# Expert weights in four consecutive rows per partition, with two places of double size

## The chip, the cores and the metric

The kernel runs on one core of one Trainium2 chip. The metric is the device time of one execution in microseconds (us). Three runs of the kernel before are shown, and one profiled execution, from which every duration below is taken.

## The reference, cut to what matters

Two networks are chained. The first has two layers; each has a mixer (attention and a gated part, which are not touched here) and a mixture of experts in which every expert chooses its tokens. Layer 0 runs it on 256 latent and 256 context tokens apart, layer 1 on the latent tokens alone. The second network has two layers of attention and MLP and is not touched.

```python
def expert_choice_ffn(h, w_router, w1, w3, w2):
    n_tok, d = h.shape[1], h.shape[2]
    cap = EC_FACTOR * n_tok // N_EXPERTS
    aff = jax.nn.softmax(jnp.einsum('bnd,de->bne', h, w_router).astype(jnp.float32), axis=-1)
    gate, idx = lax.top_k(jnp.swapaxes(aff, 1, 2), cap)
    xs = jax.vmap(lambda hb, ib: hb[ib])(h, idx)
    a = jnp.einsum('becd,edf->becf', xs, w1)
    b = jnp.einsum('becd,edf->becf', xs, w3)
    y = jnp.einsum('becf,efd->becd', jax.nn.silu(a) * b, w2) * gate[..., None].astype(h.dtype)
    ...
```

There are 16 experts in each of the two layers, with w1, w3 and w2 of 1024 x 1024 floats (4 MiB) each: 2 x 16 x 3 x 4 MiB = 384 MiB that are read once. Each expert takes 32 tokens of a stream.

## The kernel before, in words

`build` chains the parts: the even mixer, `moe(0)`, the odd mixer, `moe(1)`, then the second network. All weights are loaded by `wload` (L153), which SyncE (SP) issues in program order on one queue; a load waits on SP until its place is free, and every load behind it waits too. Outside of `moe`, places are taken in turn from `self.slots`: a ring of four buffers of 8 KB per partition, and one more buffer from the second stage on.

In `moe` (L1000 to L1250) a list, `self.plan`, gives the place of each load: the four ring buffers, then buffers that the earlier stages have left (`b3`, the layer's own small rings `rb`, the six of `big`), single tiles that are not yet wanted (`early`, the two halves of a load in two tiles `om`; `spare`, the later groups' `xs`), and then the same again. A load is 1 MiB: 256 rows of an expert matrix, with two consecutive rows in each partition (`paired=True`, "(p k) n -> p k n"), so a packet is 8 KB.

Since partition p holds rows 2p and 2p+1, everything that is multiplied with these rows is put in the same order:

- `gather` (L1092) builds `xs`, the experts' tokens with the features on the partitions, by matmuls whose stationary operand is `paired(...)`: every second float of a token's row (L1097).
- `paired_gains` (L1258) brings the norm's gain and shift into the same order, by two groups of four small matmuls (L1267), each with a copy to `gb` (L1269). It stands at the start of `moe`, among the last vector operations of the router (`rstd`, L274 to L280; the logits `lgS`, L527).
- `expert` (L1111) multiplies `xs` with w1 into `pa` and with w3 into `pb` (L1121), takes silu and the product, transposes the hidden rows with stride 2 (`hps`, L1130) into `hT`, and multiplies with w2 into `py` (L1140).

In layer 0 a group of matmuls has 64 token rows and takes the 1024 columns in two halves (HF = 2); in layer 1 it has 32 rows and four quarters (HF = 4). Every float32 matmul is two records in the trace.

Of the kernel before, what the change touches and what calls it, by code (L numbers as in the profile page):

```python
# [8 lines left out]
F32 = mybir.dt.float32  # L9
# [71 lines left out]
class Net:  # L81
# [11 lines left out]
    def open(self, ctx, ring):  # L93
# [3 lines left out]
        self.slots = [(ctx.enter_context(tc.tile_pool(name="ring", bufs=ring)), "w", ring)] * ring  # L97
        self.turn = 0
        self.plan = []
# [25 lines left out]
    def load_gains(self, t, names):  # L125

        nc = self.nc
        if t:
            st = self.wk.tile([P, P], F32, tag="kz", name="gs", bufs=2)
        else:  # L130
            pool, tag, bufs = self.slots[0]
            st = pool.tile([P, 2048], F32, tag=tag, name="gs", bufs=bufs)[:, :P]
# [20 lines left out]
    def wload(self, src, kk, n, paired=False):  # L153

        slot = self.plan.pop(0) if self.plan else None
        if slot is None:
            slot = self.slots[self.turn % len(self.slots)]
            self.turn += 1
        if type(slot) is list:
            for k, t in enumerate(slot):  # L160
                self.nc.sync.dma_start(out=t, in_=src.rearrange("(p k) n -> p k n", p=P)[:, k, :])
            return slot
        if type(slot) is tuple:
            pool, tag, bufs = slot
            t = pool.tile([P, 2048], F32, tag=tag, name="w", bufs=bufs)
        else:
            t = slot
        v = t[:, :kk * n].rearrange("p (k n) -> p k n", k=kk)
        self.nc.sync.dma_start(out=v, in_=src.rearrange("(p k) n -> p k n" if paired else "(k p) n -> p k n", p=P))
        return v  # L170
# [826 lines left out]
    def moe(self, L, streams):  # L997
# [6 lines left out]
        with ExitStack() as st:  # L1004
# [10 lines left out]
            self.paired_gains(gb, L)  # L1015
            ga, b3 = gb[:, 0], gb[:, 1]
            base = self.slots
            self.slots = base + [(self.big, "b%d" % i, 1) for i in (0, 1, 2, 4, 5, 6)]
            self.slots = self.slots[:5] + [(rb[-1], "w", n[1])] * n[1] + self.slots[5:] + [(rb[0], "w", n[0])] * n[0]
            self.turn = 0  # L1020
# [88 lines left out]

            def expert(e, xs, y4, hooks={}):  # L1110
                pa = ab.tile([P, CW], F32, tag="ab", name="pa")  # L1111
                pb = ab.tile([P, CW], F32, tag="ab", name="pb")
                for dst, nm in ((pa, "exp_w1"), (pb, "exp_w3")):
                    for k0 in range(0, NK, 2):
                        if (nm, k0) in hooks:
                            hooks[nm, k0]()
                        w = self.wload(A[nm][L, e, k0 * P:(k0 + 2) * P, :], 2, D, True)
# [711 lines left out]
```

## Time and profile before

| | |
|---|---|
| median of 3 runs | 2309.74 us (2308.86 to 2312.27) |
| profiled execution | 2310.7 us |
| its span, first to last instruction | 2308.6 us |
| TensorE busy | 2054.4 us, 89% |
| VectorE, ScalarE, GpSimd busy | 43%, 32%, 9% |
| DMA, the weights' queue | 71.1% of 16 engines, 275 GB/s mean |
| granted clock, mean | 0.939 |

The experts of layer 0 run from about 293 to 741 us, those of layer 1 from about 958 to 1395 us. The table's shares are averages over stages with different limits, so the two expert stretches are read by themselves. A window's row gives each engine's busy time in it, the granted clock, the mean busy share of the 16 DMA engines (it can read slightly over 1) and the GB/s moved.

### The profile page before, as it was taken

The page shows a single profiled execution, that of the slowest core. Times are in us where ns is not written, and L with a number is a line of the kernel's source. Part 1 is how long each engine was busy: PE and PEld are TensorE (multiplying, and loading weights), DVE is VectorE, ACT ScalarE, POOL GpSimd, SP SyncE. Part 2 cuts the span into 40 slices and gives each one's busy share as a digit, 9 for nine tenths or more (in the row PEclk, how much of TensorE's full clock was granted, in tenths as well). Part 3 has the DMA queues.
Part 4 walks back from the last instruction along what each step waited for, and adds up shares of the span by engine and source line. Part 5 has one row for each costly group of instructions (what it writes and reads, how often), then busy time and mean ns, then how long its engine had stood idle before and what let it go on. Part 6 is the DMA issues. An engine that isn't in the chain of part 4 may idle for free.

```text
span 2308.6 us, 31250 instructions
## 1 busy us (share of the span) xinstructions
PE 2054.4 (89%) x12759; PEld 1340.9 (58%) x12759; DVE 987.7 (43%) x1744; ACT 747.9 (32%) x1226; POOL 206.3 (9%) x254
## 2 busy tenths in 40 slices
PE   6999899999887899786666658999999999999998
PEld 3666644433222667543222225777899888778997
DVE  4456532132211756410110105456664555566545
ACT  4345210110000444100000004665454457655443
POOL 1001000000000210000000002111111102021112
PEclk8999999999999899887786778999999999999999
DMA  8547589999999476999999996435555544355552
GB/s 327 201 154 257 220 332 421 418 418 421 422 421 398 157 258 244 354 420 421 420 421 421 421 421 235 147 104 162 174 186 179 201 164 142 124 171 177 183 199 74
DMA packets 156746, 634.10 MB, mean 275 GB/s; under 512 B 12270, under 2 KB 16955, under 8 KB 101691
## 3 DMA queue, kind: packets, MB, share of 16 engines
q1 hardware_dynamic: 155354, 630.53, 71.1%
q8 instruction: 100, 1.64, 0.3%
q10 hardware_dynamic: 1248, 1.58, 0.2%
q14 instruction: 44, 0.35, 0.0%
HBM read 631.02 MB, written 1.05 MB: 274 GB/s over the span
## 4 chain that ended last, share of the span: by engine, by line
PE 65%; DMA 26%; DVE 5%; issue 2%; ACT 1%; POOL 1%; SPq 0%; DVEq 0%; ACTq 0%; POOLq 0%
DMA w<-in_exp_w_dram 25%; PE ps L242 8%; PE ps L244 8%; PE ps L243 8%; PE ups L1419 8%; PE acc L1419 7%; PE py L1140 3%; PE pa L1121 3%; PE pb L1121 3%; PE mod L408 2%; PE gps L1097 2%; PE S L546 2%; PE Z L1419 1%; DMA w<-in_mod_w_dram 1%; PE S L1419 1%
## 5 line engine op out<-in xcount | busy, mean ns | idle before, releaser
L182 DVE TENSOR_TENSOR wl<-w,wh 128x1024 fp32r<-128x1024 f32 (+2 forms) x333 | 409.1, 1250 | 167.2 <-ACT wh L181 158.7
L181 ACT CAST wh<-w 128x1024 fp32r<-128x1024 f32 (+2 forms) x337 | 338.1, 1027 | 171.5 <-PE acc L1419 69.6
L1121 PE MATMUL pb<-w,xs 128*32 128x256 f32 (+1 forms) x1504 | 208.7, 533 | 61.6 <-DMA w<-in_exp_w_dram 60.9
L1121 PE MATMUL pa<-w,xs 128*32 128x256 f32 (+1 forms) x1536 | 212.0, 521 | 43.2 <-DMA w<-in_exp_w_dram 42.3
L1140 PE MATMUL py<-w,ht 128*32 128x256 f32 (+1 forms) x1520 | 199.7, 515 | 41.9 <-DMA w<-in_exp_w_dram 27.6
L1126 DVE TENSOR_TENSOR sa<-sa,pb 128x512 f32<-128x512 f32 (+1 forms) x32 | 17.7, 555 | 412.7 <-PE pb L1121 359.0
L242 PE MATMUL ps<-wh,hT 128*128 128x512 f32 x468 | 187.5, 401 | 0.4 <-DVE g L1402 0.4
L243 PE MATMUL ps<-wl,hT 128*128 128x512 f32 x468 | 183.6, 392 | 0.0
L244 PE MATMUL ps<-wh,hT 128*128 128x512 f32 x468 | 183.3, 392 | 0.0
L1121 PEld LDWEIGHTS pb<-w,xs 128*32 128x32 f32 (+1 forms) x1504 | 69.3, 135 | 189.0 <-issue 88.3
L1121 PEld LDWEIGHTS pa<-w,xs 128*32 128x32 f32 (+1 forms) x1536 | 68.2, 132 | 162.1 <-issue 78.7
L1419 PE MATMUL acc<-wh,u 128*128 128x512 f32 x512 | 160.3, 390 | 0.0
L1140 PEld LDWEIGHTS py<-w,ht 128*32 128x32 f32 (+1 forms) x1520 | 67.4, 131 | 155.2 <-issue 72.9
L1125 ACT ACTIVATE sa<-pa 128x512 f32<-128x512 f32 (+1 forms) x32 | 15.7, 490 | 431.5 <-PE pa L1121 431.3
L1419 PE MATMUL ups<-hh,wl 128*128 128x256 f32 x512 | 145.0, 283 | 0.0
L1419 PE MATMUL ups<-hh,wh 128*128 128x256 f32 x512 | 145.0, 283 | 0.0
L1419 PE MATMUL ups<-hl,wh 128*128 128x256 f32 x512 | 144.9, 283 | 0.0
L1154 DVE TENSOR_TENSOR y<-py,om 32x512 f32<-32x512 f32 (+1 forms) x96 | 53.2, 554 | 174.8 <-PE py L1140 172.9
L1419 PEld LDWEIGHTS acc<-wh,u 128*128 128x128 f32 x512 | 96.1, 188 | 19.6
L242 PEld LDWEIGHTS ps<-wh,hT 128*128 128x128 f32 x468 | 88.2, 188 | 21.9 <-issue 2.1
L1419 PE MATMUL acc<-wl,u 128*128 128x512 f32 x256 | 99.8, 390 | 0.0
L244 PEld LDWEIGHTS ps<-wh,hT 128*128 128x128 f32 x468 | 88.3, 189 | 18.9
(446 smaller groups left out, 3327.1 us busy)
## 6 DMA issues: line engine op xcount, KB each, us to landing
w<-in_exp_w_dram SPq DMA_DIRECT2D x380, 1024.0 KB, 19.8
w<-in_w_in_dram SPq DMA_DIRECT2D x60, 1024.0 KB, 5.2
w<-in_mod_w_dram SPq DMA_DIRECT2D x48, 1024.0 KB, 6.0
w<-in_w_up_dram SPq DMA_DIRECT2D x32, 1024.0 KB, 5.3
w<-in_w_down_dram SPq DMA_DIRECT2D x32, 1024.0 KB, 6.7
w<-in_w_o_dram SPq DMA_DIRECT2D x8, 1024.0 KB, 5.1
w<-in_ev_w_in_dram SPq DMA_DIRECT2D x7, 1024.0 KB
w<-in_od_w_in_dram SPq DMA_DIRECT2D x6, 1024.0 KB, 7.2
```

Source lines behind the costliest of these rows:

```text
L181: nc.scalar.copy(vh, raw)
L182: (eng or nc.vector).tensor_tensor(vl, raw, vh.bitcast(F32), op=ALU.subtract)
L242: nc.tensor.matmul(ps[:, :nb], a, wh[:, cols], start=j == 0, stop=False)
L243: nc.tensor.matmul(ps[:, :nb], a, wl[:, cols], start=False, stop=False)
L244: nc.tensor.matmul(ps[:, :nb], b, wh[:, cols], start=False, stop=j == kt - 1)
L408: nc.tensor.matmul(ps[32 * j:32 * j + 32, :], self.sc[:, k, :], w[:, 0, j * 512:(j + 1) * 512], start=k == 0, stop=k == NK - 1, skip_group ...
L546: nc.tensor.matmul(Sv[e][:, :nk], a[:, t * P:(t + 1) * P], b, start=i == 0, stop=masks is None and i == len(qk[e]) - 1, skip_group_check=True)
L1097: nc.tensor.matmul(ps[:, s * nj + j, :], self.paired(streams[s][:, t, :], k + j), OH[s, t][:, g * P:(g + 1) * P], start=t == 0, stop=t == ...
L1121: nc.tensor.matmul(dst[h * T:(h + 1) * T, :], xs[:, k0 + kk, e % 4, :], wv[:, h * CW:(h + 1) * CW], start=k0 + kk == 0, stop=k0 + kk == NK ...
L1140: nc.tensor.matmul(py[n * T:(n + 1) * T, :], a, w[:, kk, n * CW:(n + 1) * CW], start=c == 0, stop=c == NK - 1, skip_group_check=True)
L1154: nc.vector.tensor_tensor(y4[s][r:r + 32, n * CW:(n + 1) * CW], py[p0:p0 + 32, :], late["m5"][s][r:r + 32, n * CW:(n + 1) * CW], op=ALU.mult)
L1419: nc.tensor.matmul(ps, a, b, start=start, stop=stop, skip_group_check=True)
```

## The change

- The ring is one tile. Two double-size places, `self.wide`, lie over its four buffers; a load to one of them takes 2 MiB in one go, with four consecutive rows in each partition, so a packet is 16 KB.
- Each expert matrix half (512 rows) is one `wquad`: either one load to a wide place, or two loads of 1 MiB to two other places, each with two of the partition's four rows: pieces of 8 KB, 16 KB apart in memory.
- `quads_of` pairs the other places in the order of the list; an odd one is kept and paired with the next narrow place, behind the wide ones that stand between.
- Everything multiplied with these rows follows the new order: the stationary operand of the gather takes every fourth float (`quad_cols`, 192 matmuls), the hidden transposes take stride 4 in layer 0 and 2 in layer 1, and in layer 1 the moving operand of w1 and w3 is read in pairs of floats out of every four (`hid_cols`, 1024 matmuls). `quad_gains` has two copies, 16 matmuls with 32 columns of the identity, and two copies.

Of the weight loads, 52 are wide (28 in layer 0, 24 in layer 1) and 276 are narrow, beside the half loads to `om`. In layer 0 the two wide loads stand, counted in MiB of expert weights from the layer's first, at 0, 18, 32, 48, 62 and then every 12 or 14 up to 178. The last loads of both layers are narrow.

```diff
-        self.slots = [(ctx.enter_context(tc.tile_pool(name="ring", bufs=ring)), "w", ring)] * ring
+        ring_t = ctx.enter_context(tc.tile_pool(name="ring", bufs=1)).tile([P, ring * 2048], F32, name="ring")
+        self.slots = [ring_t[:, i * 2048:(i + 1) * 2048] for i in range(ring)]
+        self.wide = [ring_t[:, i * 2048:(i + 2) * 2048] for i in range(0, ring, 2)]
...
+    def wquad(self, src):
+
+        place = self.quads.pop(0)
+        v = src.rearrange("(p k) n -> p k n", k=4)
+        if type(place) is not tuple:
+            t = place.rearrange("p (k n) -> p k n", k=4)
+            self.nc.sync.dma_start(out=t, in_=v)
+            return [t[:, k, :] for k in range(4)]
+        rows = []
+        for slot in place:
+            k = len(rows)
+            if type(slot) is list:
+                for i, t in enumerate(slot):
+                    self.nc.sync.dma_start(out=t, in_=v[:, k + i, :])
+                rows += slot
+            else:
+                t = self.slot_tile(slot).rearrange("p (k n) -> p k n", k=2)
+                self.nc.sync.dma_start(out=t, in_=v[:, k:k + 2, :])
+                rows += [t[:, i, :] for i in range(2)]
+        return rows
+
+    @staticmethod
+    def quads_of(units):
+
+        odd = None
+        for u in units:
+            if type(u) not in (tuple, list) and u.shape[1] == 4096:
+                yield u
+            elif odd is None:
+                odd = u
+            else:
+                yield odd, u
+                odd = None
...
-                                nc.tensor.matmul(ps[:, s * nj + j, :], self.paired(streams[s][:, t, :], k + j),
+                                nc.tensor.matmul(ps[:, s * nj + j, :], self.quad_cols(streams[s][:, t, :], k + j),
...
+            def hid_cols(w, h):
+
+                if HF == 2:
+                    return w[:, h * CW:(h + 1) * CW]
+                return w.rearrange("p (q c r b) -> p q r c b", q=2, r=2, b=2)[:, h // 2, h % 2]
...
-                    for k0 in range(0, NK, 2):
...
-                        w = self.wload(A[nm][L, e, k0 * P:(k0 + 2) * P, :], 2, D, True)
...
+                    for c in range(NK):
...
+                        if c % 4 == 0:
+                            w = self.wquad(A[nm][L, e, c * P:(c + 4) * P, :])
+                        for h in range(HF):
+                            nc.tensor.matmul(dst[h * T:(h + 1) * T, :], xs[:, c, e % 4, :], hid_cols(w[c % 4], h),
+                                             start=c == 0, stop=c == NK - 1, skip_group_check=True)
...
-                    nc.tensor.transpose(ps[:, j, :], self.paired(h, j), self.ident)
+                    nc.tensor.transpose(ps[:, j, :], h[:, j:j + nj * (P - 1) + 1:nj], self.ident)
...
-            self.plan = self.slots[:6] + early + self.slots[6:] + spare + wide
-            for n in (2, 2, 1):
-                self.plan += self.slots + spare[:n]
+            units = self.wide + base[4:] + early_ring[:1] + early + early_ring[1:] + big + late_ring + spare + wide
+            for n in (2, 1 if L else 2, 1):
+                units += cycle + spare[:n]
+            self.quads = list(self.quads_of(units + cycle * 16))[:16 * 6]
...
-    def paired(x, k):
-
-        c = k // 2 * 2 * P + k % 2
-        return x[:, c:c + 2 * P - 1:2]
+    def quad_cols(x, c):
+
+        c = c // 4 * 512 + c % 4
+        return x[:, c:c + 4 * P - 3:4]
...
+        st = out.rearrange("p a k s -> p (a k s)").rearrange("p (u a q s) -> p u a q s", u=4, a=2, q=2)
         for i, src in enumerate((ga, self.mod_cols(L, 3))):
-            st = src.rearrange("p (a h) s -> p h a s", h=2)
-            ps = self.tp.tile([P, 2, NK // 2, 2], F32, tag="t", name="pgp")
-            for b in range(2):
-                for h in range(2):
-                    nc.tensor.matmul(ps[h * 64:h * 64 + 64, b], self.ident[:, b:P:2], st[:, h], start=b == 0,
-                                     stop=b == 1, skip_group_check=True)
-            nc.vector.tensor_copy(out[:, i].rearrange("p (a b) s -> p b a s", b=2), ps)
+            nc.vector.tensor_copy(st[:, :, i], src.rearrange("p (q u) s -> p u q s", q=2))
+        ps = self.tp.tile([P, 4, 2, 2, 2], F32, tag="t", name="pgp")
+        for i in range(4):
+            for u in range(4):
+                nc.tensor.matmul(ps[u * 32:u * 32 + 32, i], self.ident[:, i:P:4], st[:, u], start=i == 0, stop=i == 3,
+                                 skip_group_check=True)
+        for i in range(2):
+            nc.vector.tensor_copy(out[:, i].rearrange("p (q c) s -> p c q s", q=2), ps[:, :, i])
```

How the order of the work moves is shown at two places. The first is SP's queue in layer 0, where the ring and the places of the `xs` tiles are refilled for the second time. Before (`w` are the places, numbered as they are taken; w_2945 is the place of an `xs` tile, w_2951 to w_3001 are the four ring buffers):

```order
L169 DMA w_2916<-in_exp_w3_dram 128x2048 [waits DMAHW0_49,PE_49]
L169 DMA w_2922<-in_exp_w3_dram 128x2048 [waits DMAHW1_49,PE_49]
L169 DMA w_2928<-in_exp_w3_dram 128x2048 [waits DMAHW2_49,PE_49]
L169 DMA w_2945<-in_exp_w2_dram 128x2048 [waits DMAHW3_49,PE_49]
L169 DMA w_2951<-in_exp_w2_dram 128x2048 [waits DMAHW4_49,PE_49]
L169 DMA w_2957<-in_exp_w2_dram 128x2048 [waits DMAHW5_49,PE_49]
L169 DMA w_2963<-in_exp_w2_dram 128x2048 [waits DMAHW6_49,PE_49]
L169 DMA w_3001<-in_exp_w1_dram 128x2048 [waits DMAHW7_49,PE_49]
```

And after the change (`ring_64` with 128x4096 is a wide load):

```order
L185 DMA w_2876<-in_exp_w3_dram 128x2048 [waits DMAHW5_49,PE_49]
L185 DMA w_2878<-in_exp_w3_dram 128x2048 [waits DMAHW6_49,PE_49]
L174 DMA ring_64<-in_exp_w2_dram 128x4096 [waits DMAHW7_49,PE_49]
L174 DMA ring_64<-in_exp_w2_dram 128x4096 [waits DMAHW0_49,PE_49]
L185 DMA w_2949<-in_exp_w1_dram 128x2048 [waits DMAHW1_49]
L185 DMA w_2951<-in_exp_w1_dram 128x2048 [waits DMAHW2_49,PE_49]
```

The place of the `xs` tile (w_2945 before) is now taken by w_2949: it is behind both wide loads, and its only wait is for the completion counter of an earlier load.

The second place is VectorE at the start of `moe` in layer 0, between the last steps of `rstd` and the router's logits `lgS`. Before:

```order
L1269 COPY gb<-pgp 128x2x4x2
L280 TENSOR_SCALAR rs_y<-rs_t,rs_y 128x1
L279 SCALAR_TENSOR_TENSOR rs_t<-rs_y,rs_v 128x1
L1269 COPY gb<-pgp 128x2x4x2
L280 TENSOR_SCALAR rsn<-rs_t,rs_y 128x1
L527 SCALAR_TENSOR_TENSOR lgS<-lgt,rsn,lgc 128x16
```

And after:

```order
L310 TENSOR_SCALAR rs_y<-rs_t,rs_y 128x1
L309 SCALAR_TENSOR_TENSOR rs_t<-rs_y,rs_v 128x1
L1304 COPY gb<-pgp 128x4x2x2
L310 TENSOR_SCALAR rsn<-rs_t,rs_y 128x1
L1304 COPY gb<-pgp 128x4x2x2
L557 SCALAR_TENSOR_TENSOR lgS<-lgt,rsn,lgc 128x16
```

The first copy out of the small matmuls has moved down by two operations, and both stand behind the whole group of 16 matmuls; the logits still come after them.

## Rows read from the trace of the kernel before

**Rows 1.** The page's fourth part, the chain that ended last, by line.

```profile
DMA w<-in_exp_w_dram 25%; PE ps L242 8%; PE ps L244 8%; PE ps L243 8%; PE ups L1419 8%; PE acc L1419 7%; PE py L1140 3%; PE pa L1121 3%; PE pb L1121 3%; PE mod L408 2%; PE gps L1097 2%; PE S L546 2%; PE Z L1419 1%; DMA w<-in_mod_w_dram 1%; PE S L1419 1%
```

**Rows 2.** DMA issues of the page: count, KB each, median us to landing.

```profile
w<-in_exp_w_dram SPq DMA_DIRECT2D x380, 1024.0 KB, 19.8
```

**Rows 3.** Windows: length, busy PE, PEld, DVE, ACT, POOL, clock, DMA share, GB/s.

```profile
480.00:730.00 250.00, 218.43 (x936) 70.33 (x932) 56.47 (x84) 16.05 (x25) 0.00 (x0) 0.99 1.01 421
1010.00:1390.00 380.00, 246.34 (x2512) 96.39 (x2512) 44.38 (x95) 15.50 (x35) 0.00 (x0) 0.75 1.01 420
...
1815.00:1819.00 4.00, 4.00 (x20) 3.30 (x19) 3.67 (x4) 2.21 (x3) 0.67 (x1) 1.00 1.05 402
1500.00:1800.00 300.00, 298.33 (x1711) 251.39 (x1711) 178.08 (x228) 159.08 (x231) 46.71 (x46) 1.00 0.49 164
...
9.00:13.00 4.00, 3.39 (x9) 1.69 (x10) 2.29 (x11) 1.69 (x3) 0.00 (x0) 1.00 1.02 430
```

**Rows 4.** The chain of waits at the end of layer 0's experts.

```profile
720.99 19.85 DMA w<-in_exp_w_dram
```

**Rows 5.** Waits of SP's queue, 293 to 480 us: us in total, times, longest.

```profile
SPq L169 <- PE pa L1121: 72.8, 26, 16.7
```

**Rows 6.** Windows of layer 0's first part, columns as in rows 3.

```profile
293.00:345.20 52.20, 51.90 (x266) 23.62 (x268) 14.29 (x28) 8.15 (x16) 1.01 (x2) 1.00 0.86 340
293.00:450.50 157.50, 155.61 (x806) 70.75 (x808) 35.97 (x70) 20.47 (x44) 1.01 (x2) 1.00 0.96 394
```

**Rows 7.** Waits of SP's queue, 1010 to 1400 us.

```profile
SPq L169 <- DMA w<-in_exp_w_dram: 318.0, 148, 8.3
```

**Rows 8.** Timeline of SP's queue, expert loads: start, us, count.

```profile
295.25 48.62 SPq L169 DMA_DIRECT2D w<-in_exp_w_dram  x18
316.57 0.33 SPq L169 DMA_DIRECT2D w<-in_exp_w_dram  x1
333.96 0.33 SPq L169 DMA_DIRECT2D w<-in_exp_w_dram  x1
343.54 0.33 SPq L169 DMA_DIRECT2D w<-in_exp_w_dram  x1
345.25 0.33 SPq L169 DMA_DIRECT2D w<-in_exp_w_dram  x1
295.25 152.95 SPq L169 DMA_DIRECT2D w<-in_exp_w_dram  x60
450.64 0.33 SPq L169 DMA_DIRECT2D w<-in_exp_w_dram  x1
959.69 0.33 SPq L169 DMA_DIRECT2D w<-in_exp_w_dram  x1
962.33 0.33 SPq L169 DMA_DIRECT2D w<-in_exp_w_dram  x1
```

**Rows 9.** Window after a load into an empty queue, columns as in rows 3.

```profile
316.50:330.00 13.50, 13.50 (x73) 5.34 (x68) 6.94 (x13) 0.59 (x1) 0.00 (x0) 1.00 0.93 365
```

**Rows 10.** Window at the start of layer 1's experts, columns as in rows 3.

```profile
959.60:962.30 2.70, 2.70 (x31) 1.97 (x27) 0.41 (x1) 0.46 (x1) 0.00 (x0) 0.89 0.88 285
```

**Rows 11.** Timeline of layer 0's gains and logits: start, us, engine, operation.

```profile
274.73 0.41 PE L1267 MATMUL pgp<-gain,ident 128*64 128x8 f32 x8
275.88 0.17 DVE L1269 COPY gb<-pgp 128x16 f32<-128x16 f32 x1
276.21 0.23 DVE L527 SCALAR_TENSOR_TENSOR lgS<-lgt,rsn,lgc 128x16 f32<-128x16 f32 x1
```

**Rows 12.** Weight loads by shape (count, busy, mean ns), and gather matmuls.

```profile
L1097 PEld LDWEIGHTS gps<-OH,xc 128*128 128x128 f32 x96 | 12.7, 196 | 4.9 <-issue 4.9
L1176 PEld LDWEIGHTS cmb<-xs,om 128*128 128x128 f32 x48 | 8.1, 188 | 19.4 <-issue 8.7 <-DVE xs L1166 3.0 <-ACT xs L1165 2.9
...
297.90 1.11 PE L1097 MATMUL gps<-OH,xc 128*128 128x128 f32 x8
```

**Rows 13.** Second-projection matmuls of layer 1 by shape, 980 to 1390 us.

```profile
L1121 PE MATMUL pb<-w,xs 128*32 128x256 f32 x950 | 88.1, 508 | 52.2 <-DMA w<-in_exp_w_dram 52.2
```

More of the change, by code (lines that the diff above doesn't have):

```diff
@@ L130, in load_gains @@
         else:
-            pool, tag, bufs = self.slots[0]
-            st = pool.tile([P, 2048], F32, tag=tag, name="gs", bufs=bufs)[:, :P]
+            st = self.slots[0][:, :P]
         r, where = 0, {}
@@ L151, in load_gains, with wload @@
         return turn
[L153 to L162, printed above, removed]
+    def wload(self, src, kk, n):
+        slot = self.slots[self.turn % len(self.slots)]
+        self.turn += 1
+        t = self.slot_tile(slot)
+        v = t[:, :kk * n].rearrange("p (k n) -> p k n", k=kk)
+        self.nc.sync.dma_start(out=v, in_=src.rearrange("(k p) n -> p k n", p=P))
+        return v
@@ L163, in wload, with slot_tile @@
+    def slot_tile(self, slot):
         if type(slot) is tuple:
             pool, tag, bufs = slot
[L165 to L170, printed above, removed]
+            return pool.tile([P, 2048], F32, tag=tag, name="w", bufs=bufs)
+        return slot
@@ L1014, in moe @@
             gb = act.tile([P, 2, NK, 2], F32, name="gb")
-            self.paired_gains(gb, L)
+            self.quad_gains(gb, L)
             ga, b3 = gb[:, 0], gb[:, 1]
             base = self.slots
-            self.slots = base + [(self.big, "b%d" % i, 1) for i in (0, 1, 2, 4, 5, 6)]
-            self.slots = self.slots[:5] + [(rb[-1], "w", n[1])] * n[1] + self.slots[5:] + [(rb[0], "w", n[0])] * n[0]
-            self.turn = 0
+            big = [(self.big, "b%d" % i, 1) for i in (0, 1, 2, 4, 5, 6)]
+            late_ring, early_ring = [(rb[0], "w", n[0])] * n[0], [(rb[-1], "w", n[1])] * n[1]
+            cycle = self.wide + base[4:] + early_ring + big + late_ring
             R = 2 * ns
@@ L1113, in expert @@
                 for dst, nm in ((pa, "exp_w1"), (pb, "exp_w3")):
[L1114 to L1123 removed]
+                    for c in range(NK):
+                        if (nm, c) in hooks:
+                            hooks[nm, c]()
+                        if c % 4 == 0:
[3 more added lines that the diff above has]
+                                             start=c == 0, stop=c == NK - 1, skip_group_check=True)
                 h = wk.tile([P, CW], F32, tag="sa", name="sa")
@@ L1133, in expert @@
                 py = yp.tile([P, CW], F32, tag="md", name="py")
-                for k0 in range(0, NK, 2):
-                    w = self.wload(A["exp_w2"][L, e, k0 * P:(k0 + 2) * P, :], 2, D, True)
-                    for kk in range(2):
-                        c = k0 + kk
-                        a = hT[:, c % nj, (c // nj) * T:(c // nj + 1) * T]
-                        for n in range(HF):
-                            nc.tensor.matmul(py[n * T:(n + 1) * T, :], a, w[:, kk, n * CW:(n + 1) * CW], start=c == 0,
-                                             stop=c == NK - 1, skip_group_check=True)
+                for c in range(NK):
+                    if c % 4 == 0:
+                        w = self.wquad(A["exp_w2"][L, e, c * P:(c + 4) * P, :])
+                    a = hT[:, c % nj, (c // nj) * T:(c // nj + 1) * T]
+                    for n in range(HF):
+                        nc.tensor.matmul(py[n * T:(n + 1) * T, :], a, w[c % 4][:, n * CW:(n + 1) * CW], start=c == 0,
+                                         stop=c == NK - 1, skip_group_check=True)
                 if "last" in hooks:
```

11 lines of the change are left out of this document (2 added, 9 removed).

## The prediction

> **What bounds the kernel now.** I read the page first, for the chain that ended last by line. Its largest entry is the landing of expert weights, 25% of the span, ahead of every matmul line [rows 1]. All of it comes from 380 loads of 1 MiB on SP's queue, each 19.8 us from issue to landing [rows 2]. Next I cut the two expert stretches into windows, to see which engine is full where. In layer 0, from 480 to 730 us, TensorE is busy 218.43 of 250 us and the DMA share is 1.01 at 421 GB/s; in layer 1, from 1010 to 1390 us, TensorE is busy 246.34 of 380 us and DMA is again at 1.01 and 420 GB/s [rows 3]. The chain of waits ends layer 0 on a weight load that starts at 720.99 and lands 19.85 us later [rows 4]. So both stretches are bounded by transfers, and only two things move their ends: the price of a byte, and time in which the queue is empty.
>
> The queue's own waits show where it can run empty. Between 293 and 480 us SP waits for TensorE, to release places: 72.8 us on the first expert matmul line alone, in 26 waits [rows 5]. In this stretch TensorE is full and the queue is thin: the DMA share is 0.86 up to 345.20 us and 0.96 up to 450.50 us [rows 6]. In layer 1 SP waits for the queue itself, 318.0 us in 148 waits [rows 7], so there a late release is covered, except at the stretch's start.
>
> 0.2% of the median is 4.6 us, about what a measurement of this kernel can tell from no change.
>
> **Part 1, wide loads: bytes get cheaper.** 52 loads of 2 MiB replace 104 MiB of the 1-MiB loads, with 16-KB packets for 8-KB ones. No row has a 16-KB data packet. I fit a price per packet from two saturated windows. 2-KB packets at a share of 1.05 and 402 GB/s take 1.05 x 16 x 2048 B / 402 = 85.6 ns each on their engine; 8-KB packets at 1.01 and 421 GB/s take 314.4 ns [rows 3]. The line through both has 37.2 ns per KB and 9.3 ns per packet. A wide load has 8 packets fewer on each of 16 engines than two narrow loads, so it saves 8 x 9.3 = 75 ns. Bounds: nothing, if the 9.3 ns belongs to small packets; and 26 ns per packet, 0.21 us a wide load, if the unsaturated 2-KB window (0.49 at 164 GB/s, 97.9 ns a packet) gives the slope [rows 3]. I take 75 ns, since those windows are full as the expert stretches are. In all 52 this would be 3.9 us, but only where the queue is full: 20 loads behind the second gap of layer 0 (below), 1.5 us, and 22 in layer 1 after its first two, 1.65 us.
>
> The narrow loads now write 8-KB pieces out of rows 16 KB apart. The nearest row is the modulation weights, 8-KB pieces from rows 24 KB apart: 430 GB/s from 9 to 13 us [rows 3]. I take nothing for the pitch.
>
> **Part 2, wide loads: releases come later.** A narrow place is refilled when its two rows are read; a wide place waits for the last reader of four rows, and SP's queue stands behind it. The order shows at layer 0's second refill that one narrow place, which has long been free (it waits for no engine in the new order), is issued behind two wide loads.
>
> Before, 18 loads are out by 343.87 us, and the next one goes at 345.25 [rows 8]. Up to 345.20 us the engines have moved 340 GB/s x 52.20 us = 16.93 MiB [rows 6]. Of the 18, the one issued at 333.96 is now the deferred one, and that of 343.54 is the first half of the second wide load, which waits for the reader that releases 345.25 [rows 8]. So 16 MiB are out at 345.25, and the queue runs dry (16.93 - 16) x 2.49 us = 2.3 us ahead of it. A restart costs something too: SP issued into a queue that had run dry at 316.57 us, and in the next 13.50 us 365 GB/s moved [rows 8, 9]; against 421 that is 1.8 us lost. The first gap thus makes transfers 4.05 us late.
>
> Second refill of this kind: before, 60 loads are out by 448.20 us and 59.18 MiB have moved at 450.50 [rows 6, 8]. After, 58 are out until 450.64 issues two wide ones. 58 MiB had moved by 447.6 before, so with the lag the queue is dry at 451.6; 450.64 plus the restart's 1.75 us is 452.4, so the lag becomes 4.8 us. At later refills the lag itself keeps the queue from running dry, since places are then freed by matmuls that wait for data. What is behind the waiting SP is only other weight loads; TensorE is behind them, and from 480 us on it waits for data, so the lag is paid in full. Layer 0: 4.8 - 1.5 = **+3.3 us**.
>
> Layer 1: the first reuse of the ring goes out at 959.69 us before, and its neighbour at 962.33 [rows 8], with the DMA share already at 0.88 between them [rows 10]. A wide load needs both, so transfers are 2.64 us late. After that some six loads are outstanding and nothing more is lost: 2.64 - 1.65 = **+1.0 us**.
>
> **Part 3, the router's gains.** Before, two groups of matmuls (the first 8 records in 0.41 us from 274.73 on, so 51 ns a record) have a vector copy behind each, the second copy at 275.88, and the router's logits follow at 276.21 [rows 11]. After, 16 matmuls (32 records, 1.64 us) start after two more copies and end no earlier than 274.73 + 1.64 = 276.4; two copies and the operation between them in the new order, about 0.17 us each as the copy there has it [rows 11], stand before the logits, at 276.9. VectorE works in order, so the logits and all behind them wait 0.7 us (between 0.2, if 32 columns cost half of 64, and 0.8). Router, gather and the first expert matmul stand in a chain, and the releases of part 2 shift with it. Twice 0.7: **+1.4 us**.
>
> **Part 4, strided operands.** The gather's stationary operand goes from every second float to every fourth (192 matmuls); the hidden transposes from 2 to 4 in layer 0, and in layer 1 the moving operand of the first two projections is read in pairs of floats. Stride 2 loads in 196 ns where packed weights take 188 [rows 12], so I take nothing for stride 4, and the price if not is rival B's. In layer 1 TensorE is free 134 us of 380 [rows 3]; those matmuls take 508 ns [rows 13] and would have to become some 80% longer before they bound: nothing, with the idle time as cover.
>
> [...]
>
> **The sum.** 3.3 + 1.0 + 1.4 = +5.7 us on the profiled execution of 2310.7 us (span 2308.6 and 2.1 around it), that is 2316.4. The median of the runs is 1.0 lower, so against it 2309.74 + 5.7 = **2315.4 us**, 0.25% slower.
>
> **Rivals.**
>
> A, on the other side: the packet price is the loose one, 26 ns, so every wide load in a full queue saves 0.21 us. For it: the 2-KB row at share 0.49 [rows 3]. Against it: the full 2-KB rows give 9.3 ns. With the lags as above, 4.8 + 2.64 + 1.4 - 42 x 0.21 = 0: 2309.7. Should the queue hold more than I counted and not run dry, 52 x 0.21 = 10.9 against 1.4 gives -9.5: 2300.2. The point at which it decides is 8.84 / 42 = 0.21 us a wide load with both gaps, 0.03 us with none; in between, a gain of over 4.6 us needs 0.12 us a load without the gaps.
>
> B, stride 4 doubles the weight load: 196 ns becomes about 390. Eight gather records follow each other in 1.11 us, 139 ns each, so the loads overlap matmuls already and a doubled one cannot be hidden whole [rows 12]. Each of layer 0's 256 gather records then takes up to 139 ns more, 36 us in the stretch where TensorE is full; I take half, 18 us: 2315.4 + 18 = 2333. For it: that so little stands beside a gather's load. Against it: stride 2 costs 8 ns.
>
> C, the rows do not move as 16-KB packets, or these cost as much per byte: nothing is saved, 5.7 + 3.15 = +8.9 us, 2318.6. The 2-KB row against the 8-KB row (402 against 421 GB/s [rows 3]) speaks against it. [...]
>
> **How the numbers follow.** Forecast 0.48; its own range is 2312 to 2319, the lag of layer 0 between 2 and 5 us and the router's bounds, and it splits 0.27 slower, 0.21 within 0.2% (up to 2314.4). A 0.27: 0.15 faster, 0.12 within. B 0.10 and C 0.11, both slower. 0.04 is left for gains and lags that cancel, within 0.2%. So faster 0.15, same 0.37, slower 0.48. The range goes from 2303, inside A, to 2321, above C with the router's upper bound; it leaves out B and A's far end.
>
> **What the profile after would show.** Right: new stretches with a DMA share under 1.0 near 340 to 349 and 447 to 453 us, and near 961 us; SP waiting longer on the matmul lines before 345 us; about 422.5 GB/s in the window of layer 0 from 480 to 730 us; the logits at about 276.9 us; weight loads of the gather at 188 to 200 ns. Wrong: over 425 GB/s in the full windows (A), gather weight loads near 390 ns (B), the packet count of the weight queue not smaller by 52 x 128 (C), or first- and second-projection matmuls of layer 1 that are longer and TensorE no longer waiting for data there.

## The result and the profile after

The changed kernel takes 2345.99 us (median of 4 runs, 2341.04 to 2347.68), the kernel before in the same comparison 2311.01 us (2308.86 to 2313.04): a ratio of 1.0155, 95% interval 1.014 to 1.017. It is 1.55% slower, some 36 us, where 0.25% was predicted; the time lies above the range.

All of it is lost in layer 0. Taking a layer from its first w1 matmul to the start of its last w2 matmul, in the profiled executions: layer 0 went from 293.2..742.2 (449.0 us) to 296.4..781.3 (484.9 us), and layer 1 from 437.9 to 439.7 us. What stands between the two layers and what stands behind them is some 2 us shorter each, and the start is 3 us later; the probe below has the program of before up to there and starts at 296.1 too, so the start's 3 us are scatter of the earlier stages.

The windows of the kernel after, with the columns of [rows 3]; the first is layer 1's, and the four of layer 0 answer to [rows 6]:

```profile
1010.00:1390.00 380.00, 266.05 (x2823) 124.53 (x2825) 52.83 (x113) 18.33 (x41) 0.00 (x0) 0.78 1.01 422
296.00:345.00 49.00, 48.92 (x230) 23.91 (x230) 12.10 (x23) 7.08 (x14) 0.35 (x1) 1.00 0.79 312
345.00:450.00 105.00, 99.50 (x427) 52.41 (x424) 17.06 (x33) 7.92 (x18) 0.00 (x0) 0.97 0.90 363
450.00:480.00 30.00, 28.28 (x123) 17.85 (x124) 5.90 (x13) 3.71 (x9) 0.00 (x0) 1.00 0.61 216
480.00:500.00 20.00, 18.37 (x86) 7.16 (x84) 2.11 (x4) 1.41 (x3) 0.00 (x0) 1.00 0.83 317
```

TensorE is nearly as busy as before, but the DMA engines are not. Before, from 345 to 480 us:

```profile
345.00:480.00 135.00, 130.20 (x664) 56.32 (x662) 26.49 (x49) 13.50 (x30) 0.00 (x0) 1.00 1.01 418
```

After the change the share falls to 0.61, and the queue is full only from 500 us on (1.01 at 424 GB/s from 500 to 730 us). At 421 GB/s, the rate of [rows 3], the four rows of layer 0 have lost 12.7, 14.5, 14.6 and 4.9 us (length x (1 - rate / 421)), 46.7 us together; before, the window from 293 to 345.20 lost 10 us [rows 6] and almost nothing was lost behind it. The difference, 36 us, is the whole loss.

From 296 to 480 us SP waits for TensorE alone, 163.2 us in all. Why TensorE, which so sets the releases in this stretch, is later, stands in its weight loads by shape, 330 to 730 us (count, busy, mean ns; the answer to [rows 12]):

```profile
L1127 PEld LDWEIGHTS gps<-OH,xc 128*128 128x128 f32 x96 | 23.9, 328 | 5.7 <-issue 5.7
L1127 PEld LDWEIGHTS gps<-OH,xl 128*128 128x128 f32 x96 | 23.7, 327 | 15.3 <-ACT xs L1136 8.0 <-issue 7.3
...
L1209 PEld LDWEIGHTS cmb<-xs,om 128*128 128x128 f32 x48 | 7.8, 188 | 17.3 <-ACT xs L1198 4.6 <-DVE xc L1214 3.7 <-issue 3.2
```

The gather's load went from 196 to 328 ns, while the packed one is at 188 as before. The timeline has eight gather records in about 2 us where [rows 12] had 1.11:

```profile
290.77 2.07 PE L1127 MATMUL gps<-OH,xc 128*128 128x128 f32 x8
...
294.50 1.97 PE L1127 MATMUL gps<-OH,xc 128*128 128x128 f32 x8
```

Between the two starts lie 16 records, so 233 ns each. In the kernel before, the next eight after those of [rows 12] start 0.94 us behind them, 117 ns each:

```profile
298.84 1.11 PE L1097 MATMUL gps<-OH,xl 128*128 128x128 f32 x8
```

The DMA issues of the page show that the change does what it says (answer to [rows 2]), and the packets of the weight queue fell from 155354 to 147866, by 52 x 144: 128 of data for each wide load, and 16 of 4 bytes, of which every load has as many:

```profile
w<-in_exp_w_dram SPq DMA_DIRECT2D x276, 1024.0 KB, 20.0
ring<-in_exp_w_dram SPq DMA_DIRECT2D x52, 2048.0 KB, 23.4
```

### The profile page after: what moved, and what is told of

The parts are those of the page before. It is cut to its first block, busy times and chain, and to the rows that moved or that the text cites. A ratio compares the mean times of both kernels' runs of the same rounds, so it can differ in the third digit from the quotient of the medians.

```text
span 2345.5 us, 31208 instructions
## 1 busy us (share of the span) xinstructions
PE 2090.9 (89%) x12787; PEld 1385.6 (59%) x12791; DVE 986.9 (42%) x1748; ACT 748.3 (32%) x1226; POOL 207.9 (9%) x254
## 3 DMA queue, kind: packets, MB, share of 16 engines
q1 hardware_dynamic: 147866, 630.52, 70.0%
## 4 chain that ended last, share of the span: by engine, by line
PE 66%; DMA 25%; DVE 5%; issue 2%; ACT 2%; POOL 1%; SPq 0%; ACTq 0%; DVEq 0%; POOLq 0%
DMA w<-in_exp_w_dram 18%; PE ps L272 8%; PE ps L274 8%; PE ps L273 8%; PE ups L1454 8%; PE acc L1454 7%; DMA ring<-in_exp_w_dram 6%; PE pa L1156 4%; PE py L1173 3%; PE pb L1156 3%; PE gps L1127 3%; PE mod L438 2%; PE S L576 2%; PE Z L1454 1%; PE o L1454 1%
## 5 line engine op out<-in xcount | busy, mean ns | idle before, releaser
L212 DVE TENSOR_TENSOR wl<-ring,wh 128x1024 fp32r<-128x1024 f32 (+1 forms) x274 | 338.2, 1252 | 136.1 <-ACT wh L211 129.7
L211 ACT CAST wh<-ring 128x1024 fp32r<-128x1024 f32 (+2 forms) x278 | 280.2, 1029 | 144.3 <-PE acc L1454 56.3
L1156 PE MATMUL pb<-w,xs 128*32 128x256 f32 (+1 forms) x1136 | 155.3, 521 | 42.6 <-DMA w<-in_exp_w_dram 42.6
L1156 PE MATMUL pa<-w,xs 128*32 128x256 f32 (+1 forms) x1104 | 150.4, 505 | 21.8 <-DMA w<-in_exp_w_dram 21.7
L1173 PE MATMUL py<-w,ht 128*32 128x256 f32 (+1 forms) x1104 | 139.6, 513 | 27.7 <-DMA w<-in_exp_w_dram 18.5
L1156 PEld LDWEIGHTS pb<-w,xs 128*32 128x32 f32 (+1 forms) x1136 | 50.8, 130 | 134.2 <-DMA w<-in_exp_w_dram 63.0
L1156 PEld LDWEIGHTS pa<-w,xs 128*32 128x32 f32 (+1 forms) x1104 | 49.7, 127 | 105.1 <-issue 59.0
L1173 PEld LDWEIGHTS py<-w,ht 128*32 128x32 f32 (+1 forms) x1104 | 48.0, 132 | 105.6 <-issue 50.7
## 6 DMA issues: line engine op xcount, KB each, us to landing
ring<-in_exp_w_dram SPq DMA_DIRECT2D x52, 2048.0 KB, 23.4
```

The source lines that it names most:

```text
L211: nc.scalar.copy(vh, raw)
L212: (eng or nc.vector).tensor_tensor(vl, raw, vh.bitcast(F32), op=ALU.subtract)
L1156: nc.tensor.matmul(dst[h * T:(h + 1) * T, :], xs[:, c, e % 4, :], hid_cols(w[c % 4], h), start=c == 0, stop=c == NK - 1, skip_group_check= ...
L1173: nc.tensor.matmul(py[n * T:(n + 1) * T, :], a, w[c % 4][:, n * CW:(n + 1) * CW], start=c == 0, stop=c == NK - 1, skip_group_check=True)
```

## The experiments

Two theories stood against each other. **Stride:** the gather's stationary operand at every fourth float costs TensorE some 25 us. **Gating:** the wide loads, with their wait for four rows and the odd place issued behind them, empty the queue. Times below are medians, each compared with the kernel before on the same chip. Where a run changes the order of the features, it no longer computes the reference, but shapes and counts are the same.

### The gather's stride, taken out of the change and put into the kernel before

```diff
-  self.quad_cols(streams[s][:, t, :], k + j)
+  self.paired(streams[s][:, t, :], k + j)
```

> The changed kernel, but the gather reads its stationary operand at every second float as before, so the tokens' features come in another order than the weights' rows (this part of the computation is changed; shapes and counts are the same). Stride theory: the 256 gather records of layer 0 fall from 234 to 117 ns each, 30 us of TensorE time in the stretch where it is full, and the time falls by 25 to 32 us, to 2314 to 2321 us. Gating theory (the wide loads' four-row wait and the deferred place behind them empty the queue): the gather is not the cause, the time falls by less than 8 us, to above 2338 us.

2320.83 us, ratio 1.0045 (1.0029 to 1.0062): 25 us of the 36 are gone. The gather's weight loads are back at 196 to 199 ns. The reverse edit, in the kernel before:

> The kernel before, with the gather's stationary operand at every fourth float (the features' order no longer fits the weights' rows; nothing else changes). Stride theory: slower by 20 to 30 us, 2331 to 2341 us, with the gather's weight loads at about 330 ns. Gating theory: within 6 us of the kernel before, since its queue and its releases are as they were.

2333.85 us, ratio 1.0103 (1.0088 to 1.0118): 24 us slower by this one slice. Its weight loads of the gather and its windows:

```profile
L1097 PEld LDWEIGHTS gps<-OH,xc 128*128 128x128 f32 x96 | 23.9, 327 | 4.9 <-issue 4.9
```

```profile
296.00:345.00 49.00, 48.92 (x229) 23.63 (x228) 12.11 (x23) 6.70 (x13) 0.00 (x0) 1.00 0.78 303
345.00:450.00 105.00, 105.00 (x460) 59.17 (x460) 17.53 (x33) 8.85 (x20) 0.00 (x0) 1.00 0.91 360
450.00:480.00 30.00, 28.41 (x128) 14.20 (x124) 6.25 (x13) 4.31 (x10) 0.00 (x0) 1.00 0.90 346
```

With the loads and places of before, and TensorE at 105.00 of 105.00 us, the queue is thin (0.91, 0.90 where it was 1.01): from 293 to 480 us SP waits for TensorE alone, 168.2 us in the kernel before, so with the gather's loads at 327 ns the places come free later, and the transfers that bound the layer's end start late. Layer 1, where TensorE has idle time [rows 3], is not longer (436.9 us). In both pairs, the change with and without this slice and the kernel before with and without it, TensorE takes its groups of matmuls in the same order in the first 190 us of layer 0, so nothing but the loads' price differs there. So the stride theory holds, and gating alone explains neither run.

### What else is in the change: no wide places

The ring's four buffers are paired like the other places (`units = base[:4] + base[4:] + ...`, and the same in `cycle`).

> The changed kernel without wide places: the ring's four buffers are narrow places that are paired as the others, so all loads are 1 MiB with 8-KB pieces and a place waits for two rows. Stride theory: within 8 us of the changed kernel (2338 to 2350 us), since the gather is as slow. Gating theory: most of the loss is undone, below 2325 us.

2335.97 us, ratio 1.0117 (1.0102 to 1.0132): 9 us less than the changed kernel by the two ratios, and just under the 2338 us that the stride theory had as its lower end. The stride keeps most of the loss, but wide places cost too, twice the 4.3 us that the prediction had for them (3.3 in layer 0, 1.0 in layer 1). The same with the gather at stride 2:

> Gather at stride 2 as in the run before it (features in another order than the weights' rows) and no wide places: all expert loads are 1 MiB with 8-KB pieces. If the two costs add (25 us from the gather, 10 us from the wide places, by the runs so far), about 2311 us, 2308 to 2314. Rival: wide places cost only beside the slow gather; then as with wide places and stride 2, above 2317 us.

2311.99 us, ratio 1.0019 (1.0009 to 1.0028). The costs add: 23 to 25 us for the stride, 6 to 9 us for the wide places (1.0045 against 1.0019, 1.0155 against 1.0117), and 4 us for the rest.

### What a strided operand costs, by itself

Thirteen groups of 8 extra matmuls (16 records each in float32, 8 in bfloat16 and for the transposes), each with its own line, ahead of layer 1's experts, for instance:

```diff
+ nc.tensor.matmul(ps[:, i % 4, :], x[:, 0:4 * P - 3:4], mv, start=True, stop=True, skip_group_check=True)
```

> The kernel before with 12 groups of 8 extra matmuls ahead of layer 1's experts, each with another stationary or moving operand; the results are not used. Line theory (one element per 16 bytes halves the read of a stationary operand): float32 at stride 1 and 2 take about 117 ns a record, strides 4 and 8 about 234 ns at 128 columns and half and a quarter of that at 64 and 32 columns, stride 3 in between; bfloat16 at stride 4 is as fast as packed and at stride 8 twice as slow; a moving operand at stride 4 and the transposes at stride 4 slow down too. Rival (it is this tile, or the count of columns, not the stride): the other tile at stride 4, or 32 and 64 columns, keep the packed price per column.

The weight loads of the groups by line, 958 to 988 us (count, busy us, mean ns):

```profile
L1282 PEld LDWEIGHTS prb<-OH,xl 128*128 128x128 f32 x16 | 3.9, 335 | 0.0
L1285 PEld LDWEIGHTS prb<-OH 128*128 128x128 f32 x16 | 3.8, 329 | 0.0
L1279 PEld LDWEIGHTS prb<-OH,xl 128*128 128x128 f32 x16 | 3.8, 329 | 0.0
...
L1276 PEld LDWEIGHTS prb<-OH,xl 128*128 128x128 f32 x16 | 2.9, 261 | 0.0
...
L1288 PEld LDWEIGHTS prb<-OH,xl 128*64 128x64 f32 x16 | 2.0, 208 | 0.1
L1267 PEld LDWEIGHTS prb<-OH,xl 128*128 128x128 f32 x16 | 2.0, 196 | 0.0
L1291 PEld LDWEIGHTS prb<-OH,xl 128*32 128x32 f32 x16 | 1.7, 136 | 0.1
L1297 PEld LDWEIGHTS prb<-ident,xl 128*128 128x128 f32 x8 | 1.1, 206 | 0.1
L1300 PEld LDWEIGHTS prb<-ident,xl 128*128 128x128 f32 x8 | 0.9, 143 | 0.0
L1273 PEld LDWEIGHTS <-c 128*128 128x128 bf16 x8 | 0.6, 148 | 0.0
L1270 PEld LDWEIGHTS <-c 128*128 128x128 bf16 x8 | 0.6, 113 | 0.0
```

L1267 is float32 at stride 2 (196 ns), L1276 stride 3 (261), L1279 stride 4 (329), L1282 stride 8 (335), L1285 stride 4 of another tile (329): from 8 to 16 bytes between two floats' starts the load takes longer, and at 32 hardly longer still. By busy time for 16 records this is 2.0, 2.9, 3.8 and 3.9 us, so a record at stride 4 takes 1.9 times one at stride 2. In bfloat16, 8 bytes apart take 113 ns and 16 bytes apart 148. The packed group stood first, at a granted clock of 0.68 of full speed, and does not compare.

A moving operand suffers in the same way: 16 records with a packed stationary operand and a moving one at stride 4 are busy for 3.9 us, those of stride 2 stationary and packed moving for 2.0:

```profile
L1294 PE MATMUL prb<-xl,ident 128*128 128x128 f32 x16 | 3.9, 410 | 0.0
...
L1288 PE MATMUL prb<-OH,xl 128*64 128x128 f32 x16 | 2.2, 289 | 0.0
L1267 PE MATMUL prb<-OH,xl 128*128 128x128 f32 x16 | 2.0, 281 | 0.0
L1291 PE MATMUL prb<-OH,xl 128*32 128x128 f32 x16 | 2.0, 276 | 0.0
L1297 PE MATMUL prb<-ident,xl 128*128 128x128 f32 x8 | 1.1, 283 | 0.0
...
L1300 PE MATMUL prb<-ident,xl 128*128 128x128 f32 x8 | 1.0, 272 | 0.0
L1273 PE MATMUL prb<-c 128*128 128x128 bf16 x8 | 0.7, 226 | 0.0
...
L1270 PE MATMUL prb<-c 128*128 128x128 bf16 x8 | 0.6, 219 | 0.0
```

Three parts of the expectation missed. With fewer stationary columns at stride 4 little or nothing is lost beside 128 moving ones: 16 records take 2.2 us with 64 columns and 2.0 with 32, as at stride 2 with 128. A transpose at stride 4 takes 1.1 us for 8 against 1.0 packed, although its load reads 206 against 143 ns; so the hidden transposes of the change cost next to nothing, as predicted. And bfloat16 at stride 8 is not twice as slow as at stride 4: its load takes 1.3 times as long, and its 8 matmuls 0.7 us against 0.6.

### Why wide places cost 6 us at stride 2

Each wide load as two 1-MiB loads into the same place, order and deferral kept:

```diff
-            self.nc.sync.dma_start(out=t, in_=v)
+            for k in (0, 2):
+                self.nc.sync.dma_start(out=t[:, k:k + 2, :], in_=v[:, k:k + 2, :])
```

> Gather at stride 2 (features in another order than the weights' rows), and each wide load as two 1-MiB loads into the same place: order of the places and deferral stay, packets are 8 KB, and a load waits for two rows instead of four. If the four-row wait makes the wide places dear: 2311 to 2316 us. If it is the deferral of the odd place behind them: 2320 to 2326 us, the packet saving lost on top.

2312.52 us, ratio 1.0020 (1.0010 to 1.0029): in the median as without wide places, so most of the cost comes in when 2 MiB go as one. The trace does not clear the deferral, though. From 25 to 65 us after the first w1 matmul of layer 0, without wide places, with real wide loads (the run of 2320.83 us) and with the split:

```profile
317.00:357.00 40.00, 40.00 (x208) 16.94 (x206) 13.52 (x24) 3.76 (x8) 0.00 (x0) 1.00 1.00 411
```

```profile
321.60:361.60 40.00, 40.00 (x208) 16.89 (x204) 13.52 (x24) 3.80 (x8) 0.00 (x0) 1.00 0.97 383
```

```profile
321.50:361.50 40.00, 40.00 (x207) 16.89 (x204) 13.51 (x24) 3.82 (x8) 0.00 (x0) 1.00 0.97 383
```

The split loses 40 x (1 - 383 / 421) = 3.6 us here, as the real wide loads do, and 1.0 us is lost without wide places, although each of its loads waits for two rows only. What it shares with the real wide loads is the order: the load that SP issues 40.7 us after the layer's start without wide places goes at 52.4 us, behind both wide places. Layer 0 is 453.2 us long in this run's profiled execution and 448.9 in the other's. Why the medians do not show these 4 us is open.

That 2 MiB go as one has two sides: the load waits for the readers of four rows (SP stands 67.1 us in 8 waits for TensorE ahead of the wide loads, 297 to 480 us in the run of 2320.83 us), and the four rows have one landing, 23.4 us behind the issue in the kernel after where a 1-MiB load takes 20.0. Two more runs split them by letting the halves of a place change roles at each use:

```diff
+            f = self.turns2[i] = 2 - self.turns2[i]
+            for k, o in ((0, f), (2, 2 - f)):
+                self.nc.sync.dma_start(out=t[:, o:o + 2, :], in_=v[:, k:k + 2, :])
```

> As the run with each wide load split in two 1-MiB loads (gather at stride 2, features in another order than the weights' rows), but the halves of a wide place change roles at each use, so that the first half goes where the last rows were read: SP waits for the last of the four rows' readers, as for a wide load, and then issues both halves; rows 0 and 1 still land, and can be used, ahead of rows 2 and 3. If the late release is what makes a wide place dear: 2317 to 2322 us, as with real wide loads. If it is the landing (no row can be used before 2 MiB are there): 2310 to 2314 us, as with the plain split.

2315.22 us, ratio 1.0032 (1.0018 to 1.0045). The other run has `((2, 2 - f), (0, f))` in that line:

> The counterpart of the run with the late release: each wide load as two 1-MiB loads (gather at stride 2, features in another order than the weights' rows), each going out as soon as its own two rows' readers are done, but rows 2 and 3 go first and rows 0 and 1, which are needed first, second, so that no row of the place can be used before all 2 MiB are there. If the landing is what makes a wide place dear: 2317 to 2322 us, with the queue thin again between 440 and 460 us (share under 0.8). If it is the release: 2310 to 2314 us and a full queue there.

2316.53 us, ratio 1.0030 (1.0020 to 1.0041). Neither median reaches the 1.0045 of real wide loads, and neither interval stands clear of the plain split's, so the times do not show what each side costs; the expectations, which had one of them carry all, both missed. In the profiled executions layer 0 takes 453.2 us with the split, 453.0 with the late release, 457.1 with the late landing and 460.3 with real wide loads. There the late release by itself adds nothing. What each does to the queue is seen at 440 to 460 us. In order: real wide loads, the split, late release, late landing:

```profile
440.00:460.00 20.00, 18.28 (x98) 8.37 (x96) 5.56 (x12) 3.72 (x9) 0.00 (x0) 1.00 0.65 247
```

```profile
440.00:460.00 20.00, 18.61 (x98) 8.39 (x94) 6.05 (x13) 3.72 (x9) 0.00 (x0) 1.00 1.01 421
```

```profile
440.00:460.00 20.00, 18.36 (x98) 8.39 (x96) 4.23 (x11) 3.71 (x9) 0.00 (x0) 1.00 1.00 406
```

```profile
440.00:460.00 20.00, 18.28 (x98) 8.34 (x96) 5.56 (x12) 3.71 (x9) 0.00 (x0) 1.00 0.88 339
```

The hole is there in the two runs whose rows land late. What TensorE waited for just ahead of it, 345 to 480 us, with real wide loads, late landing and late release:

```profile
L1127 PE MATMUL gps<-OH,xl 128*128 128x128 f32 x88 | 14.1, 297 | 6.3 <-ACT xs L1136 6.3
```

```profile
L1131 PE MATMUL gps<-OH,xl 128*128 128x128 f32 x88 | 14.1, 298 | 4.4 <-ACT xs L1140 4.4
```

```profile
L1131 PE MATMUL gps<-OH,xl 128*128 128x128 f32 x88 | 14.0, 294 | 0.6 <-ACT xs L1140 0.6
```

In the first two, TensorE stands 6.3 and 4.4 us before two gathers, for ScalarE, which writes the gathered tokens (`xs`) out of `gps`. With real wide loads the trace puts ScalarE's own wait down to the landing of a weight load:

```profile
411.27 1.51 ACT L1136 ACTIVATE xs<-gps,gb 128x128 f32<-128x128 f32 x4 [23.95 <-DMA w<-in_exp_w_dram]
```

But it starts 0.82 us after VectorE's first write of `xs`, and in the split, the late release and the late landing it does so too, 0.81 to 0.82 us behind, where the trace names VectorE. That write stands on VectorE behind four operations on `py`, which wait for TensorE's w2 matmuls; in the kernel after, these four start at 421.90 us behind a wait of 7.19, the write at 424.72, and ScalarE at 425.53. What differs is the order of TensorE's own work. With real wide loads, and then with the split:

```profile
400.50 7.09 PE L1173 MATMUL py<-w,ht 128*64 128x512 f32 x32 [0.78 <-DVE ht L291]
412.13 0.80 PE L1127 MATMUL gps<-OH,xl 128*128 128x128 f32 x2 [4.54 <-ACT xs L1136]
```

```profile
405.12 1.94 PE L1157 MATMUL pa<-ring,xs 128*64 128x512 f32 x8
406.99 0.50 PE L1128 MATMUL gps<-OH,xc 128*128 128x128 f32 x2
408.12 0.50 PE L1128 MATMUL gps<-OH,xl 128*128 128x128 f32 x2 [0.63 <-ACT xs L1137]
```

In the split, the late release and the run without wide places, eight w1 matmuls (`pa`) stand between w2's matmuls and the gather that has to wait; with real wide loads and with the late landing none do, so TensorE waits. So the landing of the rows is not the only thing that differs between these runs, and no run separates it from TensorE's order. What follows can be seen: in the run with real wide loads SP stands from 445.0 to 457.1 us ahead of a wide load, while the queue runs thin.

### Wide loads only where transfers bound

Still at stride 2, with the ring narrow for the first 62 MiB of layer 0 and the first three rounds of layer 1:

```diff
-                units += cycle + spare[:n]
+                units += base[:4] + cycle[2:] + spare[:n]
```

> Gather at stride 2 (features in another order than the weights' rows), with the ring's buffers as four narrow places for the first 62 MiB of layer 0 and the first 70 or so of layer 1, and as two wide places from there on, where transfers bound. If wide places cost only where TensorE sets the releases, and 16-KB packets save some 80 ns a wide load where transfers do (some 35 loads): 2306 to 2310 us, 2 to 4 us under the run without wide places. If they cost wherever they stand: 2314 us or more.

2312.39 us, ratio 1.0016 (1.0007 to 1.0025): no better than without wide places, and between the two expectations. The row from 480 to 730 us has the saving, 423 GB/s where it is 421 without wide loads, which is 1.2 us of 250; and the hole at 440 to 460 us has taken it back. SP stands there from 437.7 to 449.8 us ahead of a wide load, where the run without wide places issues four ring loads from 440.0 to 450.0; 62 MiB was too early:

```profile
440.00:460.00 20.00, 16.72 (x90) 7.89 (x86) 4.71 (x11) 3.72 (x9) 0.00 (x0) 1.00 0.73 276
480.00:730.00 250.00, 214.79 (x924) 69.80 (x922) 57.24 (x85) 16.66 (x26) 0.00 (x0) 0.99 1.01 423
```

Then a version that keeps the reference's result: gather, gains, w1 and w3 as before, and only w2 in quads, with `plan` entries "wide" for w2 alone and the ring as one tile.

> A version that computes the reference: w1, w3, the gather and the gains as in the kernel before (two rows per partition, stride 2), and only w2 in quads, with four rows per partition; the ring is one tile, narrow for the first 6 experts of layer 0 and 2 of layer 1, and two wide places for w2 from there to the last expert but one: 44 wide loads. Packet theory: 44 x 0.08 = 3.5 us faster than the kernel before, 2305 to 2308 us. Rival: the ring as one tile with fixed places, or the four-row release, costs as much or more: 2309 to 2316 us.

2315.03 us, ratio 1.0035 (1.0022 to 1.0047): slower, and the share is 0.63 at 440 to 460 us. This hole has another cause, since the first wide load of layer 0 goes at 463.4 us, behind it: the plan now keeps the ring's buffers for w2, and SP stands from 438.3 to 453.5 us for the place of a 1-MiB load, while in the next run four ring loads go in this time:

```profile
441.97 10.37 SPq L166 DMA_DIRECT2D ring<-in_exp_w_dram  x4
```

Later still, and with the last expert's loads kept off the ring:

> The version that computes the reference with only w2 in quads, its wide places from the tenth expert of layer 0 (108 MiB) and the third of layer 1 on, and the last expert's loads kept off the ring: 12 + 26 wide loads, all where transfers bound. If the loss of the first version of this kind was the empty queue at 440 to 460 us of layer 0 and the ring held into the odd mixer: layer 0 as in the kernel before less 1 us, layer 1 shorter by 2 to 3 us, in all 2304 to 2308 us against about 2309. Rival (four-row places cost where transfers bound too): 2311 us or more.

2309.92 us against 2307.55, ratio 1.0007 (0.9998 to 1.0016): no difference, between the two expectations. The hole is gone:

```profile
440.00:460.00 20.00, 18.36 (x94) 8.30 (x92) 4.20 (x10) 3.71 (x9) 0.00 (x0) 0.96 1.01 419
```

but 38 wide loads at some 80 ns are 3 us, and they do not show in the time: layer 1 took 435.9 us where the kernel before took 437.9, and layer 0 451.1 where it took 449.0. No version here beats the kernel before.

### The remaining 4 us

The run without wide places and at stride 2 is 0.19% over the kernel before, though in its profiled execution neither layer is longer (448.9 and 435.7 us against 449.0 and 437.9). One suspect, the ring as one tile with parts in turn, alone in the kernel before:

> The kernel before with its ring as one tile whose four parts are taken in turn, and nothing else changed. The run without wide places at stride 2 was 0.19% (4.4 us) slower than the kernel before. If that is the one-tile ring: 2311 to 2313 us. If it is the rest of the change (the gains, the pairing of places): within 1.5 us of the kernel before.

2311.32 against 2308.48 us, ratio 1.0008 (0.9999 to 1.0017). It may carry some of it; the interval holds both answers. This part stays open.

## Why the prediction was wrong, point by point

**Part 4, strided operands, failed, and it is the largest step: nothing was taken for the gather's stride 4, and it costs 23 to 25 us.** The argument was the nearest row, stride 2 at 196 against 188 ns [rows 12]. But the step lies between stride 2 and stride 4: 196, 261 and 329 ns at strides 2, 3 and 4 in the probe. That the load doubles, from 196 to about 390 ns, was rival B's supposition, given one chance in ten; no row showed it, and no run does: the load takes 328 ns, 1.7 times as long. Its cost came out larger than B had it: the records are 116 ns longer (233 against 117), 256 x 116 = 30 us of TensorE time at most, of which 24 reach the end; 18 had been taken for it. The other operands of part 4 went as predicted: the hidden transposes' weight loads are at 214 ns on average where they were at 206, and layer 1's matmuls whose moving operand is read in pairs of floats are no longer (495 and 447 ns in places outside the ring against 526 and 504 before, from 1010 to 1390 us). That the forecast said slower is owed to the wide places, the smaller part of the 36 us.

**Part 2, release, had the right sign, was too small, and is shown by its mechanism only in part.** The first gap is there, 3.6 us in the rows above where 4.05 had been worked out. But two loads were counted for it, one that is deferred and one that waits for four rows, and the split has the same gap with the deferral alone. The second gap was put at 0.8 us more, with "at later refills the lag itself keeps the queue from running dry"; at stride 2 the row from 440 to 460 us lost 20 x (1 - 247 / 421) = 8 us. The release times were taken from the trace of before, as if TensorE would keep its pace and its order of work, while it stands 6.3 us before gathers; and only the release of four rows was counted, not that four rows must land before one is used. Whether the landing or the other order makes TensorE wait stays open. Together with the saving, wide places cost 6 to 9 us, not 4.3.

**Part 1, the packet price, was right.** 75 ns a wide load was taken. The packets in the trace of the kernel after, 1010 to 1390 us, show the price directly: an 8-KB packet took 314.4 ns and a 16-KB packet 618.8, on average, so 10 ns are saved in each, 80 ns a wide load. The window of layer 1 reads 422 GB/s in all five runs with wide loads there and 420 or 421 in the other nine. Rival A's 26 ns a packet and rival C's nothing are both out. It is only that 3 us are small beside the rest, and no run shows them in its time.

**Part 3, the router's gains, had the wrong sign.** The 16 matmuls were counted at the 51 ns a record of 64 columns; they took 0.66 us for 32 records:

```profile
277.85 0.66 PE L1301 MATMUL pgp<-gb,ident 128*32 128x8 f32 x32
```

```profile
278.91 0.23 DVE L557 SCALAR_TENSOR_TENSOR lgS<-lgt,rsn,lgc 128x16 f32<-128x16 f32 x1
```

From the first of them to the logits it is 1.06 us, against 276.21 - 274.73 = 1.48 before [rows 11]: 0.4 us gained where 0.7 was charged. Two things were missed. The 51 ns held the length of the last record, 204 ns in both kernels: from start to start it is (0.41 - 0.204) / 7 = 29 ns with 64 columns and (0.66 - 0.204) / 31 = 15 ns with 32. And the second group of before had stood 0.28 us for the first one's copy, a wait that one group does not have.

**Layer 1** was predicted at +1.0 us; it measured 439.7 against 437.9, and 439.3 at stride 2, while runs without any wide place gave 435.7 to 437.9. The sign fits; the scatter is as large as the term.

## What to carry to other kernels

In these runs a float32 operand of 128 columns, stationary or moving, cost nearly twice as much at stride 4 (16 records 3.9 us, where those of stride 2 stationary and packed moving took 2.0), and a stationary one at stride 2 loaded in 196 ns where a packed one took 188. Before a layout is changed for the sake of DMA packets, look at what stride it leaves on TensorE, and whether TensorE is what frees the buffers there. A row at one stride says nothing of the next; give a step between them a price and a real chance, or measure it first. Larger loads saved little here, where packets were 8 KB already (some 80 ns for 2 MiB), and the places for them cost 6 to 9 us in the change: they deferred another load (383 GB/s against 411 in the first gap), and in the version with w2 alone in quads they kept the ring from other use (a share of 0.63 from 440 to 460 us). And before two runs are compared for one cause, look whether each engine still does its work in the same order.

## What the runs showed that was not expected

- A float32 stationary operand of 128 columns loads in 196 ns at stride 2, 261 at stride 3, 329 at stride 4 and 335 at stride 8; a transpose at stride 4 loses 0.1 us in eight, and beside 128 moving columns a stationary operand at stride 4 loses 0.2 us in 16 records with 64 columns and nothing with 32.
- At most 30 us more of TensorE's work in layer 0 came out as 24 us of the kernel, although that layer ends on transfers: TensorE frees the places in its first 200 us, and what the queue loses there is not made up, since from 600 us on it moves 421 GB/s in the kernel before and with the gather at stride 4 alike.
- With real wide loads instead of split ones, TensorE's gathers and w1 matmuls stand in another order, and it waits 6.3 us before gathers instead of 0.6.
